# Seven half-block products over 12 instead of 8 of the 22 inner chunks of a down projection, and two weight parts queued behind the last sum of squares

## The chip, the cores and the metric

The kernel runs on one core of a Trainium2 chip. The metric is device time in microseconds (us); three runs of the kernel before gave a median of 2041.5 us (2040.48 to 2044.54). Engines are named as the profile names them: PE is TensorE (matmuls), PEld its loading of stationary operands, DVE is VectorE, ACT ScalarE, POOL GpSimd, SP SyncE, which here only issues transfers. Each engine works through its own queue in order, and so does each queue of transfers.

## The reference

An encoder trunk of two layers on 512 positions with 1024 features, in float32:

```python
for i in range(DEPTH):
    h = h + 0.5 * swiglu(rmsnorm(h, norm_ffn1[i]), ffn1_w_gate[i], ffn1_w_up[i], ffn1_w_down[i])
    hn = rmsnorm(h, norm_mix[i])
    if i % 2 == 0:
        h = h + ab_mixer(hn, ...)     # windowed and dilated attention
    else:
        h = h + c_mixer(hn, ...)      # 2-D neighbourhood attention
    h = h + 0.5 * swiglu(rmsnorm(h, norm_ffn2[i]), ffn2_w_gate[i], ffn2_w_up[i], ffn2_w_down[i])
    gate = jax.nn.sigmoid(rmsnorm(h, norm_ple[i]) @ w_ple_gate[i])
    h = h + gate * (p[i] @ w_ple_proj[i])
return rmsnorm(h, norm_final)

def swiglu(x, w_gate, w_up, w_down):          # inner width 2816 = 22 x 128
    return (silu(x @ w_gate) * (x @ w_up)) @ w_down
```

The last line of `swiglu` holds the down projection, which there are four of: 22 inner chunks of 128 rows go into 8 output chunks of 128 features, over 512 positions.

## The kernel before

Activations lie with features on the partitions, in chunks of 128 x 512. A float32 matmul is made of three in the format fp32r: each operand is split into a high part (a copy by ACT, L149) and a low part (the difference, by DVE, L150), and high x high, high x low and low x high are added up in PSUM. Weights come in units of 128 x 1024 (8 chunks) and pass through three rings of buffers: five raw ones (`wr`), four for high parts (`wh`), four for low parts (`wl`). A unit's parts can be written when TensorE is done with the unit four places before; a raw unit can be fetched when the parts of the one five places before are made. There are 8 buffers `tmp` of 128 x 512, 62 (`ACTS`) activation tiles `act`, and PSUM banks in pools: three `mm`, two `sc`, two `tr`, one `ob`. A planner lays each engine's queue out ahead of the run, by program order among what it takes to be ready, and sets all waits.

The trunk is TensorE's work from end to end: gate and up projections (`pair_front` for the first four pairs, `pair`, then `pair_fast`, in half-block products of its own), `down`, a mixer, and so on.

**Load phase.** `setup` starts the first norm. `pair_front` for m = 0 of the first feed-forward multiplies chunk by chunk as the input arrives, makes the weight parts of the second pair ahead, and then takes the squares and their sum (`norm_square`: a square on ACT, L207; a sum into `ssq`, on DVE in this first norm, L214). From the sum `stat` makes the column of factors (L221 on PE, L223 on DVE, L224 on POOL), and `spread` and ACT (L240, L248) make R of it, which every eviction (L281, L283) and `halves` (L314 and on) multiply by. The parts of the third pair (m = 2) are made by `unit` like all others.

**Feed-forward.** For each of 22 pairs the product r = silu(gate) * up is split into parts `a[m]`; for m < 8 r itself is also written to DRAM (`raw`, a POOL transfer, L408).

**Down.** Output chunks go in pairs (m, m+1). The first pair is `plain`: units of 8, 8 and 6 inner chunks, each chunk three matmuls of 512 columns (L438 to L440). While it runs, `inner_sums` makes, for k = 0 to 3, four differences (L515) of halves of chunk k and chunk k+4 fetched back from DRAM, and splits them; one result takes the place of the right half of `a[k]`. The three pairs that follow take inner chunks 0 to 7 by a two-by-two block scheme (inner chunks k and k+4, output chunks m and m+1, left and right 256 columns) that needs seven products instead of eight, each of 4 chunks x 3 matmuls of 256 columns (L476 to L478), and chunks 8 to 21 by `plain` units of 8 and 6. `inner_weights` makes the sums of weights for the seven products (L529 to L533) and four units of parts. The seven products come first in each pair; L482 to L494 join their results, then come the plain units, which add to the two banks of the outputs, and `evict` (L443) adds a bank into h, stores h to DRAM (`kept`, L444) and calls `norm_chunk`: the split of h for the next phase (L199, L200), and square and sum (L207, and L214 on POOL). For output chunks 3, 4, 5 (`LATER`) that norm is put off: in the last pair, between the seven products and the plain units, h is fetched again from `kept` (L430) and normed then.

Of the kernel before, what the change touches and what calls it, by code (L numbers as in the profile page):

```python
# [9 lines left out]
F32 = mybir.dt.float32  # L10
# [26 lines left out]
SEVEN = 4  # L37
LATER = 3, 4, 5
UP_AT = 3
LEAD = 6  # L40
ACTS = 62
# [6 lines left out]
class Trunk:  # L48
# [113 lines left out]
    def unit(self, src, cols=UNIT, lo_eng=None):  # L162

        nc = self.nc
        raw, hi, lo = self.unit_tiles()
        nc.sync.dma_start(raw[:, :cols], src)
        self.split(raw[:, :cols], hi[:, :cols], lo[:, :cols], lo_eng)
        return hi, lo
# [35 lines left out]
    def norm_square(self, c):  # L204
# [7 lines left out]
        else:  # L212
            eng = nc.vector if c == KC - 1 or self.k == 0 else nc.gpsimd
            eng.tensor_tensor(self.acc, self.acc, sq, op=ALU.add)  # L214
# [37 lines left out]
    def pair_front(self, w, m, first, ahead):  # L252
# [3 lines left out]
        for j in range(2):  # L256
            u = self.ahead.pop(0) if self.ahead else self.unit(w[:, (1 - j) * UNIT:(2 - j) * UNIT])
# [132 lines left out]
    def ffn(self, i, which, k_next):  # L390
# [8 lines left out]
        raw = self.dp.tile([2 * SEVEN, P, T], F32, name=self.nm("inner"))  # L399
        for m in range(NF):  # L400
# [6 lines left out]
            if m < 2 * SEVEN:  # L407
                nc.gpsimd.dma_start(raw[m], r)  # L408
# [9 lines left out]
    def down(self, w, a, raw, kept):  # L418

# [6 lines left out]
        later = []  # L426
# [6 lines left out]
        def plain(p, m, s, e, start):  # L433
            u = self.unit(w[m, :, s * P:e * P], (e - s) * P)
            for j, (xh, xl) in enumerate(a[s:e]):
# [4 lines left out]
                mm(p, u[1][:, c], xh, start=False, stop=s + j == NF - 1, skip_group_check=True)  # L440
# [20 lines left out]
        for m in range(2, KC, 2):  # L461
            hs = [fetched(m + j, kept) for j in range(2)]
            wa, wb, ws, wr = self.inner_weights(w[m, :, :UNIT], w[m + 1, :, :UNIT])
            M = UNIT // 2
            p1, p2, y, z = self.bank(), self.bank(), self.sbank(), self.obank()
            x11 = [(h[:, l], lo[:, l]) for h, lo in a[:SEVEN]]
            x21, x22 = [[(h[:, c], lo[:, c]) for h, lo in a[SEVEN:2 * SEVEN]] for c in (l, r)]
            t4 = [(h[:, r], lo[:, r]) for h, lo in a[:SEVEN]]
            t1, t2 = [[(h[:, c], lo[:, c]) for h, lo, _ in sums] for c in (l, r)]
            t3 = [(t[:, l], t[:, r]) for _, _, t in sums]  # L470

            def product(out, u, off, xs, start=False, stop=False):
                mm = nc.tensor.matmul
                for k, (xh, xl) in enumerate(xs):
# [950 lines left out]
```

## Time and profile before

| What | Value |
|---|---|
| median of three runs | 2041.5 us |
| time of the profiled execution | 2042.86 us |
| its span in the trace | 2041.1 us |
| mean granted TensorE clock | 0.997 |

The profile is of one execution. Its page gives the busy time of each engine, the chain of work that ended last, and groups of instructions as "line, engine, operation, output<-input, shapes xcount | busy us, mean ns | idle before, and what ended it". A timeline lists one engine's instructions with start, busy time, and in brackets the idle time before and its releaser; "x6" stands for six merged in one row. Matmuls overlap in the pipeline, so their pitch is read from starts. A table of windows gives per stretch: its length, then for PE, PEld, DVE, ACT and POOL the busy us with the count, then granted clock, share of the DMA engines, GB/s.

### The profile page before, as it was taken

What the parts mean: (1) busy time and instruction counts of PE and PEld (TensorE: products, weight loads), DVE (VectorE), ACT (ScalarE), POOL (GpSimd) and SP (SyncE); (2) the same over time, 40 slices, a digit from 0 to 9 for tenths busy, and PEclk for the clock granted to TensorE, in tenths of its full rate; (3) what the DMA queues carried; (4) which work ended last, traced back from release to release, by engine and by line L of the source; (5) the groups of instructions that cost most, each with busy time, mean ns of one, the idle gap of its engine ahead of it and who ended that gap; (6) DMA issues with size and microseconds to landing.
All of it is one profiled execution on the core that took longest, in us unless ns stands there. A gap on an engine that the chain in (4) does not pass through costs nothing.

```text
span 2041.1 us, 33721 instructions
## 1 busy us (share of the span) xinstructions
PE 2019.5 (99%) x12862; PEld 1820.6 (89%) x12862; DVE 1520.3 (74%) x2575; ACT 1056.9 (52%) x1798; POOL 260.2 (13%) x294
## 2 busy tenths in 40 slices
PE   9999999999999999999999999999999999999997
PEld 6999988878888899988888999888888889998886
DVE  7888865598766988875668888756788688888554
ACT  6555533377644555552445555434666545555242
POOL 0100011342212110000211100002000111000021
PEclk9999999999999999999999999999999999999999
DMA  7777644553425576653545775645343447665451
GB/s 212 193 188 188 181 139 157 150 104 73 100 73 165 137 195 182 170 191 124 185 150 159 192 183 158 201 125 161 109 112 102 155 134 192 184 179 165 132 193 42
DMA packets 123123, 312.94 MB, mean 153 GB/s; under 512 B 23504, under 2 KB 31184, under 8 KB 122960
## 3 DMA queue, kind: packets, MB, share of 16 engines
q1 hardware_dynamic: 104064, 253.06, 38.3%
q0 software_dynamic: 18752, 57.69, 15.0%
q8 instruction: 101, 1.65, 0.3%
q14 instruction: 62, 0.51, 0.1%
q10 hardware_dynamic: 144, 0.04, 0.0%
HBM read 274.02 MB, written 25.66 MB: 147 GB/s over the span
## 4 chain that ended last, share of the span: by engine, by line
PE 90%; DVE 3%; DMA 2%; ACT 2%; issue 1%; POOL 1%; SPq 0%; DVEq 0%; POOLq 0%; ACTq 0%
PE mm L362 6%; PE mm L361 6%; PE mm L360 6%; PE mm L174 6%; PE mm L438 6%; PE mm L439 6%; PE mm L173 6%; PE mm L440 6%; PE mm L175 6%; PE sc L362 3%; PE sc L361 3%; PE sc L360 3%; PE sc L175 3%; PE sc L173 3%; PE sc L174 3%; PE ob L360 2%
## 5 line engine op out<-in xcount | busy, mean ns | idle before, releaser
L149 ACT ACTIVATE wh<-wr 128x1024 fp32r<-128x1024 f32 (+2 forms) x455 | 466.2, 1026 | 541.5 <-PE mm L439 170.7
L150 DVE TENSOR_TENSOR wl<-wr,wh 128x1024 fp32r<-128x1024 f32 (+2 forms) x455 | 542.8, 1196 | 203.6 <-ACT wh L149 198.1
L362 PE MATMUL mm<-act,wl 128*128 128x256 f32 x1088 | 307.9, 283 | 0.0
L361 PE MATMUL mm<-act,wh 128*128 128x256 f32 x1088 | 307.9, 283 | 0.0
L360 PE MATMUL mm<-act,wh 128*128 128x256 f32 x1088 | 307.9, 283 | 0.0
L173 PE MATMUL mm<-act,wh 128*128 128x512 f32 (+1 forms) x648 | 254.4, 393 | 0.9 <-ACT act L149 0.4
L174 PE MATMUL mm<-act,wh 128*128 128x512 f32 (+1 forms) x648 | 254.2, 392 | 0.7 <-DVE act L200 0.6
L175 PE MATMUL mm<-act,wl 128*128 128x512 f32 (+1 forms) x648 | 253.3, 391 | 0.0
L361 PEld LDWEIGHTS mm<-act,wh 128*128 128x128 f32 x1088 | 208.9, 192 | 0.4
L362 PEld LDWEIGHTS mm<-act,wl 128*128 128x128 f32 x1088 | 208.9, 192 | 0.2
L360 PEld LDWEIGHTS mm<-act,wh 128*128 128x128 f32 x1088 | 208.9, 192 | 0.2
L438 PE MATMUL mm<-act,wh 128*128 128x512 f32 x512 | 199.4, 389 | 0.0
L439 PE MATMUL mm<-act,wh 128*128 128x512 f32 x512 | 199.4, 389 | 0.0
L440 PE MATMUL mm<-act,wl 128*128 128x512 f32 x512 | 199.2, 389 | 0.0
L149 ACT ACTIVATE act<-tmp 128x512 fp32r<-128x512 f32 (+1 forms) x204 | 113.7, 590 | 83.0 <-DVE tmp L515 33.1
L360 PE MATMUL sc<-act,wh 128*128 128x256 f32 x544 | 154.0, 283 | 0.0
L361 PE MATMUL sc<-act,wh 128*128 128x256 f32 x544 | 154.0, 283 | 0.0
L362 PE MATMUL sc<-act,wl 128*128 128x256 f32 x544 | 154.0, 283 | 0.0
L174 PEld LDWEIGHTS mm<-act,wh 128*128 128x128 f32 x648 | 122.2, 189 | 24.5 <-DVE act L200 2.2
L173 PEld LDWEIGHTS mm<-act,wh 128*128 128x128 f32 x648 | 121.9, 188 | 23.9 <-ACT act L199 0.8
L175 PEld LDWEIGHTS mm<-act,wl 128*128 128x128 f32 x648 | 122.1, 188 | 22.1 <-DVE wl L150 0.2
L150 DVE TENSOR_TENSOR act<-tmp,act 128x512 fp32r<-128x512 f32 (+1 forms) x200 | 125.7, 643 | 9.7 <-ACT act L149 7.7
(224 smaller groups left out, 4430.0 us busy)
## 6 DMA issues: line engine op xcount, KB each, us to landing
wr<-in_gu_dram SPq DMA_DIRECT2D x176, 512.0 KB, 4.7
wr<-in_gu_dram POOLq DMA_DIRECT2D x68, 512.0 KB, 5.5
wr<-in_dn_dram SPq DMA_DIRECT2D x64, 512.0 KB, 3.9
rb<-in_gu_dram SPq DMA_DIRECT2D x68, 256.0 KB, 3.0
wr<-in_dn_dram SPq DMA_DIRECT2D x32, 384.0 KB, 3.2
wr<-in_qk_ab_dram SPq DMA_DIRECT2D x20, 512.0 KB, 3.3
tmp<-kept SPq DMA_DIRECT2D x36, 256.0 KB, 4.1
inner<-tmp POOLq DMA_DIRECT2D x32, 256.0 KB, 3.6
```

Source lines behind the costliest of these rows:

```text
L149: self.put(self.nc.scalar.activation(hi, src, AF.Copy))
L150: self.put((lo_eng or self.nc.vector).tensor_tensor(lo, src, hi.bitcast(F32), op=ALU.subtract))
L173: mm(out, stat[0], mov[0], start=start, stop=False)
L174: mm(out, stat[0], mov[1], start=False, stop=False)
L175: return mm(out, stat[1], mov[0], start=False, stop=stop)
L360: mm(out, w[0][:, c], xs[k][0][:, x], start=start and k == 0, stop=False, skip_group_check=True)
L361: mm(out, w[0][:, c], xs[k][1][:, x], start=False, stop=False, skip_group_check=True)
L362: mm(out, w[1][:, c], xs[k][0][:, x], start=False, stop=stop and k == half - 1, skip_group_check=True)
L438: mm(p, u[0][:, c], xh, start=start and j == 0, stop=False, skip_group_check=True)
L439: mm(p, u[0][:, c], xl, start=False, stop=False, skip_group_check=True)
L440: mm(p, u[1][:, c], xh, start=False, stop=s + j == NF - 1, skip_group_check=True)
```

## The change

- `TWO` names six pairs of inner chunks: (0, 4), (1, 5), (2, 6), (3, 7), (8, 10), (9, 11). The seven products now cover inner chunks 0 to 11, with 6 chunks each. `raw` holds 12 chunks. `inner_sums` runs six times per down, for a pair once the first output pair's unit with its chunks has been issued.
- `plain` covers chunks 12 to 21, in two units of 5 (`others`).
- `inner_weights` fetches 1024 + 512 columns of both outputs (the 512 into the two buffers `rb` of `pair_fast`) and fills six units of parts instead of four.
- In the second output pair (m = 2) the plain units come first and the seven products after them; in the third and fourth pair the seven products come first, as before.
- The norm of output chunks 1 to 5 instead of 3 to 5 is put off to the last pair. `ACTS` goes from 62 to 64.
- In the load phase the parts of the third pair's two units are queued behind the last sum of squares (DVE's instructions among them; `issue_after` orders instructions on one engine).

```diff
-SEVEN = 4
-LATER = 3, 4, 5
+TWO = (0, 4), (1, 5), (2, 6), (3, 7), (8, 10), (9, 11)
+SEVEN = 12
+LATER = 1, 2, 3, 4, 5
-ACTS = 62
+ACTS = 64
...
-    def unit(self, src, cols=UNIT, lo_eng=None):
+    def unit(self, src, cols=UNIT, lo_eng=None, behind=None):
...
-        self.split(raw[:, :cols], hi[:, :cols], lo[:, :cols], lo_eng)
+        with self.tc.issue_after(behind.ins) if behind else ExitStack():
+            self.split(raw[:, :cols], hi[:, :cols], lo[:, :cols], lo_eng)
...
-            eng.tensor_tensor(self.acc, self.acc, sq, op=ALU.add)
+            self.last_sum = eng.tensor_tensor(self.acc, self.acc, sq, op=ALU.add)
...
-            u = self.ahead.pop(0) if self.ahead else self.unit(w[:, (1 - j) * UNIT:(2 - j) * UNIT])
+            u = self.ahead.pop(0) if self.ahead else self.unit(
+                w[:, (1 - j) * UNIT:(2 - j) * UNIT], behind=self.last_sum if first and m == 2 else None)
...
-            if m < 2 * SEVEN:
+            if m < SEVEN:
                 nc.gpsimd.dma_start(raw[m], r)
...
+        def others(p, m, start, stop):
+            mid = (SEVEN + NF) // 2
+            plain(p, m, SEVEN, mid, start, False)
+            plain(p, m, mid, NF, False, stop)
...
         for s in range(0, NF, 8):
+            e = min(NF, s + 8)
             for m in range(2):
-                plain(ps[m], m, s, min(NF, s + 8), s == 0)
-            if s == 0:
-                sums = [self.inner_sums(k, a, raw) for k in range(SEVEN)]
+                plain(ps[m], m, s, e, s == 0, e == NF)
+            sums += [self.inner_sums(k, k2, a, raw) for k, k2 in TWO if s <= max(k, k2) < e]
...
+        def seven(m, p1, p2, first, hs):
+
+            a11, a12, a22, s1, s2, s3, s4 = self.inner_weights(w[m], w[m + 1])
+            y, z = self.sbank(), self.obank()
             e, f, u2 = self.tmp(), self.tmp(), self.tmp()
+            product(y[:, l], a11, x11, True)
             act(e[:, l], y[:, l], AF.Copy)
+            product(p1[:, l], a12, x21, first)
+            product(p2[:, l], a22, t4, first, not first)
+            product(z[:, l], s1, t1, True, True)
+            product(y[:, r], s3, t3)
+            product(p1[:, r], s4, x22, False, not first)
+            product(y[:, l], s2, t2, False, True)
             act(u2[:, l], y[:, l], AF.Copy)
...
+        for m in range(2, KC, 2):
+            hs = [fetched(m + j, kept) for j in range(2)]
+            ps = self.bank(), self.bank()
+
+            first = m > 2
+            if first:
+                seven(m, *ps, True, hs)
             if m == KC - 2:
                 for c in later:
                     self.h[c] = fetched(c, self.kept)
                     self.norm_chunk(c)
+            for j, p in enumerate(ps):
+                others(p, m + j, not first, first)
+                if first:
+                    evict(m + j, p, hs[j])
+            if not first:
+                seven(m, *ps, False, hs)
+                for j, p in enumerate(ps):
+                    evict(m + j, p, hs[j])
...
     def inner_weights(self, w1, w2):
+        nc, dma, tt = self.nc, self.nc.sync.dma_start, self.nc.vector.tensor_tensor
+        M, G = UNIT // 2, UNIT // 4
...
+        for n, s in ((UNIT, 0), (M, UNIT)):
+            for x in (w1, w2):
+                raws.append(tile(self.wr, "wr", F32) if n == UNIT else
+                            self.tp.tile([P, T], F32, tag="rb", name=self.nm("rb"), bufs=2))
+                dma(raws[-1], x[:, s:s + n])
+        ra, rs, ra2, rs2 = raws
...
+        (ga,), (gb, b22) = parts(ra), parts(ra2, rs[:, M:])
         tt(rs[:, M:], rs[:, :M], rs[:, M:], op=ALU.add)
         tt(rs[:, :M], ra[:, :M], rs[:, :M], op=ALU.subtract)
+        (gs,) = parts(rs)
+        hi, lo = tile(self.wh, "wh", F32R), tile(self.wl, "wl", F32R)
+        self.split(rs2[:, G:], hi[:, :G], lo[:, :G])
+        tt(rs2[:, G:], rs2[:, :G], rs2[:, G:], op=ALU.add)
+        tt(rs2[:, :G], ra2[:, :G], rs2[:, :G], op=ALU.subtract)
+        self.split(rs2, hi[:, G:G + M], lo[:, G:G + M])
...
         tt(ra[:, :M], rs[:, M:], ra[:, :M], op=ALU.subtract)
         tt(ra[:, M:], ra[:, M:], ra[:, :M], op=ALU.subtract)
+        (gr,) = parts(ra)
+        tt(ra2[:, :G], rs2[:, G:], ra2[:, :G], op=ALU.subtract)
+        tt(ra2[:, G:], ra2[:, G:], ra2[:, :G], op=ALU.subtract)
+        (gr2,) = parts(ra2)
+        return (ga[:4] + gb[:2], ga[4:] + gb[2:], b22 + d22, gs[4:] + d1, gr[:4] + gr2[:2], gs[:4] + d3,
+                gr[4:] + gr2[2:])
```

More of the change, by code (lines that the diff above doesn't have):

```diff
@@ new lines, in inner_weights, with parts @@
+        raws = []
+        for n, s in ((UNIT, 0), (M, UNIT)):
[4 more added lines that the diff above has]
+        ra, rs, ra2, rs2 = raws
+        def parts(*srcs):
+            hi, lo, out, n = tile(self.wh, "wh", F32R), tile(self.wl, "wl", F32R), [], 0
+            for x in srcs:
+                c = slice(n, n + x.shape[-1])
+                self.split(x, hi[:, c], lo[:, c])
+                out.append([(hi[:, i:i + P], lo[:, i:i + P]) for i in range(c.start, c.stop, P)])
+                n = c.stop
+            return out
```

67 lines of the change are left out of this document (19 added, 48 removed).

## The prediction

> **What bounds the kernel now.** I read the page first: busy times, then the chain that ended last.
>
> ```profile
> span 2041.1 us, 33721 instructions
> PE 2019.5 (99%) x12862; PEld 1820.6 (89%) x12862; DVE 1520.3 (74%) x2575; ACT 1056.9 (52%) x1798; POOL 260.2 (13%) x294
> ...
> PE 90%; DVE 3%; DMA 2%; ACT 2%; issue 1%; POOL 1%; SPq 0%; DVEq 0%; POOLq 0%; ACTq 0%
> ...
> tmp<-kept SPq DMA_DIRECT2D x36, 256.0 KB, 4.1
> ```
>
> TensorE is busy for all but 2041.1 - 2019.5 = 21.6 us. So a matmul taken away shortens the kernel, and a wait put in front of TensorE lengthens it; work on VectorE, ScalarE or a queue counts only where TensorE comes to wait for it. Next, the first down projection by its four pairs of output chunks (window; then busy us and count of PE, PEld, DVE, ACT, POOL):
>
> ```profile
> 239.66:269.60 29.94, 29.94 (x134) 24.79 (x133) 24.39 (x45) 12.97 (x23) 0.58 (x1) 1.00 0.54 180
> 269.60:298.75 29.15, 29.15 (x169) 25.84 (x168) 17.54 (x21) 10.55 (x14) 4.68 (x4) 1.00 0.49 155
> 298.75:327.80 29.05, 29.05 (x169) 25.79 (x168) 15.09 (x19) 8.29 (x10) 1.10 (x2) 1.00 0.43 137
> 327.80:356.90 29.10, 29.10 (x170) 25.80 (x169) 18.61 (x19) 13.48 (x18) 7.43 (x6) 1.00 0.56 182
> ```
>
> TensorE never pauses here and its granted clock is 1.00. VectorE is filled to 24.39 of 29.94 us while the inner sums are made, to 15 to 19 of 29 afterwards. That is the room in which the change must put its new work. The pitch of matmuls stands in TensorE's timeline (start, busy; the starts are what counts, since busy times overlap):
>
> ```profile
> 271.04 0.28 PE L476 MATMUL mm<-act,wh 128*128 128x256 f32 x1
> ...
> 279.68 0.40 PE L438 MATMUL mm<-act,wh 128*128 128x512 f32 x1
> ...
> 298.75 0.28 PE L476 MATMUL sc<-act,wh 128*128 128x256 f32 x1
> ```
>
> From 271.04 to 279.68 lie six products of 12 half-width matmuls: 8.64/72 = 0.120 us each. From 279.68 to 298.75 lie 84 full-width ones: 19.07/84 = 0.227 us each.
>
> **Part 1, the seven products over 12 chunks.** Four more chunks for two outputs were 4 x 2 x 3 = 24 full matmuls, 24 x 0.227 = 5.45 us. They become 7 x 2 x 3 = 42 half ones, 42 x 0.120 = 5.04 us. That is 0.41 us saved per pair, and with three pairs in each of four downs 12 x 0.41 = **4.9 us off TensorE**, all of it on the path. [...]
>
> The price on the other engines, from the groups of instructions by shape:
>
> ```profile
> L150 DVE TENSOR_TENSOR wl<-wr,wh 128x1024 fp32r<-128x1024 f32 x406 | 501.4, 1237 | 184.5 <-ACT wh L149 179.0 <-PE mm L477 2.0 <-PE sc L175 1.7
> L150 DVE TENSOR_TENSOR act<-tmp,act 128x512 fp32r<-128x512 f32 x168 | 113.9, 685 | 8.5 <-ACT act L149 7.5
> L150 DVE TENSOR_TENSOR act<-tmp,act 128x256 fp32r<-128x256 f32 x32 | 13.4, 420 | 1.2 <-ACT act L149 0.2
> L515 DVE TENSOR_TENSOR tmp<-tmp,tmp 128x256 f32<-128x256 f32 x48 | 18.2, 421 | 1.6 <-DMA tmp<-inner 1.4
> ```
>
> An inner sum costs VectorE 4 x 0.42 (L515) + 2 x 0.42 + 0.69 = 3.2 us; two more per down are 6.4 us. Weights of a pair: four more sums of 256 columns (1.7 us), parts of 512, 256, 512 and 512 (0.69 + 0.42 + 0.69 + 0.69 = 2.5 us); the plain units hold 4 x 640 columns instead of 2 x 1024 and 2 x 768, at the first row's rate -1.2 us. So some +3 us in 29. In the first stretch the load would be 24.4 + 6.4 = 31 us, over 29.94; but the first pair now runs its plain part first (60 x 0.227 = 13.6 us), so there are 43.5 us for the 31, the plain units' 4 x 0.78 = 3.1 and the 3 of the weights, 37 in all. Cost taken: nothing, under the cover of VectorE's free quarter; if the sums ran late, the fourth product would wait for them (bound 6.4 us a down). ScalarE, at 13 of 30, takes its halves of the same parts. Four more stores of r per feed-forward on POOL's queue (POOL is at 13%) and four more fetches per down on SP, each ahead of weight loads that TensorE needs 20 us later: nothing. Nor do two more activation tiles cost time.
>
> **Part 2, the new join.** After the plain-first pair the next pair starts with seven products again, directly behind seven products. Its third product writes a PSUM bank that the pair before still holds until its first eviction. With three such banks, that eviction must land within two products, 36 x 0.120 = 4.3 us. The queue in front of it, from VectorE's timeline at the same place of the kernel before:
>
> ```profile
> 281.52 0.42 DVE L490 TENSOR_TENSOR tmp<-ob,tmp 128x256 f32<-128x256 f32 x1
> ...
> 283.24 0.69 DVE L494 SCALAR_TENSOR_TENSOR tmp<-tmp,tmp 128x512 f32<-128x512 f32 x1
> ...
> 289.43 0.69 DVE L443 SCALAR_TENSOR_TENSOR tmp<-mm,tmp 128x512 f32<-128x512 f32 x1 [1.99 <-PE mm L440]
> 290.76 0.69 DVE L529 TENSOR_TENSOR wr<-wr 128x512 f32<-128x512 f32 x1
> ...
> 292.03 1.79 DVE L530 TENSOR_TENSOR wr<-wr,wr 128x512 f32<-128x512 f32 x1
> ```
>
> And from ScalarE's, the copy that L490 waits for, and the first half of a norm:
>
> ```profile
> 266.52 0.71 ACT L199 ACTIVATE act<-tmp,gain 128x512 fp32r<-128x512 f32 x1
> ...
> 280.51 0.37 ACT L489 ACTIVATE tmp<-sc 128x256 f32<-128x256 f32 x1
> ```
>
> L490 to L494 take 283.93 - 281.52 = 2.4 us, the eviction 0.69, the copy with what it waits 0.5: 3.6 us, which fits by 0.7 us. If one weight part of 1.24 us gets between, it is late by 0.5 us; with the two of 512 columns as well, by 1.3. Nothing to 1.3 us per down; I take 0.2, since each queue is laid out by program order among what is ready, and evictions stand ahead of the later weights: **+0.8 us** in all.
>
> **Part 3, the end of a down.** Output chunks 1 to 5 instead of 3 to 5 have their norm put off to the last pair: a fetch from DRAM on SP, two ScalarE and one VectorE instruction, one sum on POOL each. The stretch after the last seven products shrinks from 19.07 to 13.6 us. SP's timeline in the kernel before:
>
> ```profile
> 340.33 1.30 SPq L430 DMA_DIRECT2D tmp<-kept  x2
> 345.75 0.33 SPq L166 DMA_DIRECT2D wr<-in_qk_ab_dram  x1
> 346.13 0.43 SPq L430 DMA_DIRECT2D tmp<-kept  x1
> ```
>
> The third fetch stands behind a weight load (L166) that waits for its buffer. Five fetches can stand behind three such loads. The fetch takes 4.1 us (first fence); the next phase needs chunk k only k x 24/8 x 0.227 = 0.68k us after its start, 3.4 us for chunk 5. If the fifth is issued 13 us into the 13.6, it lands at 17.1 and its parts (0.71 on ScalarE, 0.75 on VectorE) are ready at 18.6, against 13.6 + 3.4 = 17.0: 1.6 us late. If it is issued with the fourth, at 10, it is in time. TensorE can meanwhile take the first chunks of the next weight units. Nothing to 1.6 us; I take 0.2 per down, **+0.8 us**.
>
> **Part 4, the load phase.** VectorE's and TensorE's timelines:
>
> ```profile
> 17.82 4.67 DVE L214 TENSOR_TENSOR ssq<-ssq,tmp 128x512 f32<-128x512 f32 x6
> 22.41 1.22 DVE L150 TENSOR_TENSOR wl<-wr,wh 128x1024 fp32r<-128x1024 f32 x1
> 23.54 0.68 DVE L214 TENSOR_TENSOR ssq<-ssq,tmp 128x512 f32<-128x512 f32 x1
> 24.15 1.22 DVE L150 TENSOR_TENSOR wl<-wr,wh 128x1024 fp32r<-128x1024 f32 x1
> 25.37 0.16 DVE L223 TENSOR_SCALAR ms<-tr 128x4 f32<-128x4 f32 x1
> ```
>
> ```profile
> 24.28 1.05 PE L221 MATMUL tr<-ones,ssq 128*128 128x1 f32 x8 [1.00 <-DVE ssq L214]
> ...
> 26.41 0.63 PE L174 MATMUL mm<-act,wh 128*128 128x512 f32 x1
> 26.84 0.63 PE L175 MATMUL mm<-act,wl 128*128 128x512 f32 x1
> ...
> 53.39 0.50 PE L175 MATMUL sc<-act,wl 128*128 128x512 f32 x1 [0.43 <-DVE wl L150]
> ```
>
> ```profile
> 20.00:40.00 20.00, 19.00 (x83) 15.45 (x82) 15.75 (x28) 9.83 (x15) 3.22 (x4) 0.91 0.66 151
> 40.00:60.00 20.00, 19.57 (x88) 16.07 (x87) 19.82 (x33) 10.43 (x15) 1.44 (x2) 1.00 0.47 120
> ```
>
> The third pair's part at 22.41 delays the last sum by 23.54 - 22.41 = 1.1 us. TensorE idles 1.00 us for it and then runs at a pitch of 0.43 instead of 0.227 us; the clock of the slice is 0.91, so 20 x 0.09 = 1.8 us are lost. On TensorE alone up to 1.0 + 1.8 = 2.8 us could come back. But from 40 to 60 VectorE is busy 19.82 of 20, and TensorE at 53.39 waits for it; so what counts is how much earlier VectorE's own row of work starts, after L223. The matmuls between L221 and the transposes that spread R then run at 0.227, which I count as 0.6 us; L223 itself comes 1.1 us earlier if it runs ahead of the second part, and not at all if both parts, which now queue behind the last sum, come first. So VectorE gains 0.6 to 1.7 us. What TensorE gains beyond that turns into a longer wait at 53.39. Bounds: 2.8 us gained; 0.6 lost, if the longer wait brings the slow pitch again (1.8) and VectorE gains 1.2. I take the middle of 0.6 and 1.7, **-1.2 us**.
>
> **Sum.** -4.9 + 0.8 + 0.8 - 1.2 = -4.5 us. The profiled execution ran 2042.86 us, 1.8 over its span of 2041.1; by it the change gives 2038.4. The median of the runs is 2041.5, 1.4 below it, so the forecast against the median is **2037.0 us**. A measurement of this kernel can tell about 0.2%, 4.1 us, from no change; the forecast lies 0.4 us beyond that bound.
>
> **The rivals.**
> *The joins eat it (same).* Each new join is late by the 1.3 us of part 2: 4 x 1.3 = 5.2 instead of 0.8, 2041.4 us. For it: weights precede in time while the eviction is not ready; against: no wait of TensorE stands anywhere in the downs before.
> *The late norms (slower).* One mechanism: the fetches of chunks 1 to 5 go out one by one behind weight loads. If the fourth and the fifth each stand behind another load, the loads being freed every 15 x 0.227 = 3.4 us, the fifth goes out at 16.4, is ready at 22.0 and TensorE waits 5 us per down: 2037.0 - 0.8 + 20 = 2056 us. It turns the verdict once a down loses (4.5 + 0.8 + 4.1)/4 = 2.4 us. For it: the 4.5 us from the end of the second fetch's issue to the third. Against: other units' first chunks can fill in.
> *POOL slows VectorE (same or a little slower).* L530 took 1.79 us where L529 just before took 0.69; POOL began a sum at 291.56:
>
> ```profile
> 291.56 1.71 POOL L214 TENSOR_TENSOR ssq<-ssq,tmp 128x512 f32<-128x512 f32 x1 [0.58 <-ACT tmp L207]
> ```
>
> That is 1.1 more. Two more sums in the shorter last stretch are 2.2 us of VectorE per down; if all reaches TensorE, 8.8 us, 2045.8 us; VectorE's 18.61 of 29.10 speaks against. [...]
> *The load phase gives nothing (same).* The longer wait at 53.39 brings the slow pitch again: 2037.0 + 1.2 + 0.6 = 2038.8 us.
>
> **How the numbers follow.** Forecast 0.50 (its own range 2034.0 to 2038.5, of which 0.42 lies below 2037.4, the bound of faster); joins 0.20; late norms 0.12; POOL 0.08; load 0.10. Of joins and load 0.05 is faster, where the other part goes better than taken, and 0.25 the same; POOL splits into 0.05 the same and 0.03 slower. Faster 0.47, same 0.08 + 0.25 + 0.05 = 0.38, slower 0.15. The range, 2033.8 to 2043.5, goes from all of part 4 (2.8) with no join loss, 2041.5 - 4.9 - 2.8, past the joins case, and leaves out the late norms and most of the POOL case.
>
> **What would show it.** Right: half-width matmuls in the downs at 0.120, each pair 28.7 us; the first L221 near 23.2 with no wait; few waits of TensorE at the third product of the second pair. Wrong: TensorE waiting for L443's successor or for a put-off norm at the end of each down, a clock below 1.00 in slices there, or a wait at 53 us that has grown beyond 1.5 us.

## The result and the profile after

The changed kernel took 2052.2 us in the median of 6 runs (2050.7 to 2058.8), the kernel before 2042.0 beside it: ratio 1.0054, interval 1.0043 to 1.0065. It is slower by 10 us, where 4.5 us faster was forecast. First the page of the changed kernel:

```profile
span 2051.2 us, 34574 instructions
PE 2022.2 (99%) x13078; PEld 1831.3 (89%) x13078; DVE 1566.1 (76%) x2727; ACT 1079.4 (53%) x1870; POOL 266.8 (13%) x310
```

TensorE is still the path, yet it is busy for 2.7 us more with less to do, and idle for 29.0 us instead of 21.6. Its mean granted clock is 0.994 instead of 0.997, which fits busy time that grows while there is less to multiply. To find the place, cut both spans where a down begins and ends (first and last `plain` matmul) and take a table of windows over the pieces (first the stretch, then its length and TensorE's busy time). Kernel before:

```profile
0.00:239.66 239.66, 235.56 (x1692) 220.25 (x1693) 199.60 (x294) 137.12 (x211) 20.64 (x30) 0.99 0.69 188
239.66:357.03 117.37, 117.37 (x638) 102.33 (x637) 75.62 (x104) 45.32 (x66) 13.78 (x13) 1.00 0.50 163
357.03:877.55 520.52, 516.19 (x3358) 460.68 (x3356) 405.00 (x783) 298.19 (x580) 99.82 (x122) 1.00 0.52 135
...
994.92:1279.20 284.28, 283.96 (x1933) 263.74 (x1932) 222.90 (x332) 153.26 (x228) 33.19 (x36) 1.00 0.61 170
...
1396.57:1852.39 455.82, 454.12 (x3037) 416.74 (x3036) 356.09 (x698) 265.78 (x488) 37.67 (x42) 1.00 0.52 145
...
1969.76:2041.10 71.34, 60.15 (x303) 49.92 (x301) 34.58 (x56) 21.43 (x31) 13.26 (x12) 0.94 0.27 93
```

And the changed kernel:

```profile
0.00:238.18 238.18, 234.54 (x1693) 218.98 (x1693) 199.66 (x295) 137.11 (x211) 23.92 (x34) 1.00 0.70 193
238.18:354.47 116.29, 116.29 (x693) 103.97 (x691) 82.25 (x137) 47.00 (x78) 7.39 (x10) 1.00 0.53 173
354.47:878.63 524.16, 517.17 (x3357) 461.39 (x3356) 411.67 (x789) 301.67 (x586) 108.40 (x130) 1.00 0.52 138
...
994.93:1284.13 289.20, 287.21 (x1933) 265.69 (x1932) 226.61 (x336) 156.73 (x234) 41.51 (x44) 0.99 0.60 172
...
1400.42:1860.81 460.39, 455.80 (x3037) 417.73 (x3036) 361.27 (x703) 269.26 (x494) 44.16 (x50) 1.00 0.52 147
...
1977.10:2051.20 74.10, 62.35 (x303) 51.58 (x301) 37.27 (x59) 25.05 (x37) 19.68 (x16) 0.91 0.27 93
```

The four downs alike went from 117.37 to 116.29 us, busy throughout: 4 x 1.08 = 4.3 us won. The stretch ahead of the first down became 1.5 us shorter. All that turned the result lies in the four stretches behind a down, which hold the same matmuls as before: 3.64 + 4.92 + 4.57 + 2.76 = 15.9 us. The sum, -4.3 - 1.5 + 15.9 = +10.1, is the difference of the spans.

What waits there stands in the changed kernel's list of TensorE's waits (total us, times, longest):

```profile
PE tr L242 <- POOL rcol L226: 5.9, 4, 1.7
...
PE mm L176 <- DVE act L202: 2.0, 4, 1.2
PE sc L175 <- ACT act L201: 1.8, 1, 1.8
```

L201 and L202 are the split of a norm, L226 and L242 the column of factors that comes of the finished sum of squares and its spreading into R. The row of 1.8 us is behind the first down, at 359.12: there it is the split of the fourth put-off chunk itself that comes late. Behind the four downs TensorE's waits make 2.1, 2.0, 2.9 and 1.7 us, 8.7 in all (two of the rows hold waits of the load phase too); in the kernel before they make 0, 0.2, 0 and 0.8. The rest of the 15.9 shows behind the second down, in TensorE's timeline:

```profile
1003.54 0.50 PE L176 MATMUL mm<-act,wh 128*128 128x512 f32 x1 [0.27 <-DVE act L202]
...
1007.49 1.11 PE L242 MATMUL tr<-ident,rcol 128*128 128x128 f32 x4 [1.72 <-POOL rcol L226]
1008.26 0.78 PE L175 MATMUL mm<-act,wh 128*128 128x512 f32 x1
...
1009.26 0.63 PE L177 MATMUL mm<-act,wl 128*128 128x512 f32 x1
...
1013.10 0.62 PE L177 MATMUL sc<-act,wl 128*128 128x512 f32 x1
```

In the kernel before, the same matmuls of L242 (there L240) came without a wait:

```profile
1004.55 0.65 PE L240 MATMUL tr<-ident,rcol 128*128 128x128 f32 x4
```

Here there is a pause of 1.72 us, and then the next ten matmuls start every 0.43 us (1009.26 to 1013.10 are nine pitches) instead of 0.227, at half the clock (granted 0.50 from 1006.76 to 1013.59). The twelve matmuls from 1008.26 to 1013.52 take 5.26 us instead of 12 x 0.227 = 2.7, which is 2.5 us, so the pauses (2.0) and the slow piece together are most of the 4.92. Why the norms are late is seen in SP's queue at the same place:

```profile
983.65 0.39 SPq L432 DMA_DIRECT2D tmp<-kept  x1
987.05 0.33 SPq L167 DMA_DIRECT2D wr<-in_plg_dram  x1
987.47 0.38 SPq L432 DMA_DIRECT2D tmp<-kept  x1
990.45 0.33 SPq L167 DMA_DIRECT2D wr<-in_plp_dram  x1
990.88 0.40 SPq L432 DMA_DIRECT2D tmp<-kept  x1
993.85 0.33 SPq L167 DMA_DIRECT2D wr<-in_plg_dram  x1
994.22 0.42 SPq L432 DMA_DIRECT2D tmp<-kept  x1
```

The last four of the five fetches (L432) go out one by one, each behind a weight load (L167), 3.3 to 3.8 us apart; the fifth leaves 0.7 us before the down ends. Its norm and those of the last chunks then crowd VectorE and POOL (both engines' timelines):

```profile
1000.45 3.04 DVE L202 SCALAR_TENSOR_TENSOR act<-tmp,gain,act 128x512 fp32r<-128x512 f32 x2 [0.38 <-ACT act L201]
1003.41 0.68 DVE L216 TENSOR_TENSOR ssq<-ssq,tmp 128x512 f32<-128x512 f32 x1
...
999.94 2.99 POOL L216 TENSOR_TENSOR ssq<-ssq,tmp 128x512 f32<-128x512 f32 x2 [0.92 <-ACT tmp L209]
```

The last sum is done at 1004.09, 9.2 us behind the down; in the kernel before it was done at 998.48, 3.6 us behind:

```profile
997.79 0.69 DVE L214 TENSOR_TENSOR ssq<-ssq,tmp 128x512 f32<-128x512 f32 x1
```

### The profile page after: what moved, and what is told of

It is laid out like the page before. It is cut to its first block, busy times and chain, and to the rows that moved or that the text cites. A ratio compares the mean times of both kernels' runs of the same rounds, so it can differ in the third digit from the quotient of the medians.

```text
span 2051.2 us, 34574 instructions
## 1 busy us (share of the span) xinstructions
PE 2022.2 (99%) x13078; PEld 1831.3 (89%) x13078; DVE 1566.1 (76%) x2727; ACT 1079.4 (53%) x1870; POOL 266.8 (13%) x310
## 4 chain that ended last, share of the span: by engine, by line
PE 91%; DVE 3%; ACT 2%; DMA 2%; issue 1%; POOL 1%; SPq 0%; DVEq 0%; POOLq 0%; ACTq 0%
PE mm L365 6%; PE mm L364 6%; PE mm L363 6%; PE mm L175 6%; PE mm L176 6%; PE mm L177 6%; PE mm L440 4%; PE mm L441 4%; PE mm L442 4%; PE sc L365 3%; PE sc L364 3%; PE sc L363 3%; PE sc L177 3%; PE sc L176 3%; PE sc L175 3%; PE ob L365 2%
## 5 line engine op out<-in xcount | busy, mean ns | idle before, releaser
L150 ACT ACTIVATE wh<-wr 128x1024 fp32r<-128x1024 f32 (+3 forms) x455 | 454.8, 1003 | 438.5 <-DVE wr L353 81.9
L151 DVE TENSOR_TENSOR wl<-wr,wh 128x1024 fp32r<-128x1024 f32 (+3 forms) x455 | 526.6, 1162 | 160.8 <-ACT wh L150 136.5
L150 ACT ACTIVATE act<-tmp 128x512 fp32r<-128x512 f32 (+1 forms) x228 | 123.7, 578 | 110.7 <-DVE tmp L532 55.5
L440 PE MATMUL mm<-act,wh 128*128 128x512 f32 x416 | 162.0, 389 | 0.0
L441 PE MATMUL mm<-act,wh 128*128 128x512 f32 x416 | 162.0, 389 | 0.0
L442 PE MATMUL mm<-act,wl 128*128 128x512 f32 x416 | 161.8, 389 | 0.0
L151 DVE TENSOR_TENSOR act<-tmp,act 128x512 fp32r<-128x512 f32 (+1 forms) x224 | 137.6, 631 | 12.4 <-ACT act L150 8.8
```

The costliest lines, as they stand in the source:

```text
L150: self.put(self.nc.scalar.activation(hi, src, AF.Copy))
L151: self.put((lo_eng or self.nc.vector).tensor_tensor(lo, src, hi.bitcast(F32), op=ALU.subtract))
L440: mm(p, u[0][:, c], xh, start=start and j == 0, stop=False, skip_group_check=True)
L441: mm(p, u[0][:, c], xl, start=False, stop=False, skip_group_check=True)
L442: mm(p, u[1][:, c], xh, start=False, stop=stop and j == e - s - 1, skip_group_check=True)
```

## The experiments

Three theories: **A**, the number of norms put off against the length of the last products (19.1 us before, 13.6 after) sets the end, through the chain of fetches; **B**, POOL's sums of squares beside VectorE lengthen it; **C**, something else behind the down ends last, and the norms only look like it. All ratios below are to the kernel before on the same chip, with their interval. "Gaps" are the four stretches behind the downs, less those of the profiled kernel before; each is of one execution, and in other versions of the kernel before, with three chunks put off, they lie between -1.4 and +0.5, so that much is scatter.

**The load phase alone**, in the kernel before (`behind` and its use, nothing else).

> The kernel before with the load-phase edit alone. In the changed kernel the first down starts 1.48 us earlier than before (238.18 against 239.66) and nothing else changed ahead of it. Both theories: the span is 1.5 us shorter, ratio 0.9993, the first L223 (the sum over partitions) near 23.2 us, the granted clock of 20 to 40 us back at 1.00. If the gain is lost later, the time is unchanged.

2043.0 us, 1.0006 (0.9997 to 1.0015): nothing that can be told. The first stretch was 238.98 us here. But it was 238.04 in the next kernel, which lacks this edit, and 239.76 in a later one, which has it: what decides about it is told below, with part 4.

**Five chunks put off, alone**, in the kernel before:

```diff
-LATER = 3, 4, 5
+LATER = 1, 2, 3, 4, 5
```

> The kernel before with the norms of output chunks 1 to 5 instead of 3 to 5 put off; 8 chunks in the seven products, so the stretch behind the last seven products keeps its 19.07 us. Theory A (the five fetches go out one at a time, each behind the square of the chunk before in the order of the tmp buffers and so behind a weight load that waits 3.4 to 5.4 us): the fifth fetch goes out some 19 us into the stretch, TensorE loses 2 to 4 us after each down, 2042 + 8 to 16 = 2050 to 2058 us. Theory B (six sums on POOL, and VectorE beside them, do not fit into the 13.6 us of the changed kernel): with 19 us and POOL busy 7.4 of 29 us they fit, at most 1 us per down, 2042 to 2046 us.

2054.5 us, 1.0062 (1.0049 to 1.0076); gaps +1.4, +3.8, +5.1, +4.2, together 14.5 of the 15.9 us. One constant, without the new products and with the old 19.1 us, reproduces the loss. VectorE's last sum behind the second down:

```profile
998.84 3.04 DVE L200 SCALAR_TENSOR_TENSOR act<-tmp,gain,act 128x512 fp32r<-128x512 f32 x2 [0.38 <-ACT act L199]
1001.80 0.68 DVE L214 TENSOR_TENSOR ssq<-ssq,tmp 128x512 f32<-128x512 f32 x1
```

**All fetches first**, in the changed kernel, to break the chain:

```diff
 for c in later:
     self.h[c] = fetched(c, self.kept)
+for c in later:
     self.norm_chunk(c)
```

> The changed kernel with all five fetches issued ahead of the five norms instead of one fetch and one norm in turn; the work of every engine is the same. Theory A: the five fetches stand together in SP's queue, the fifth chunk lands some 10 us earlier, the 15.9 us lost after the four downs (3.6, 4.9, 4.6, 2.8) shrink to 0 to 4, so 2052 - 12 to 16 = 2036 to 2040 us. Theory B: POOL and VectorE have the same work in the same stretch, 2048 us or more.

2066.0 us, 1.0119 (1.0105 to 1.0132): worse. The fetches did leave together, but the norms then stand in a block, ahead of the weight parts:

```profile
992.22 6.43 POOL L216 TENSOR_TENSOR ssq<-ssq,tmp 128x512 f32<-128x512 f32 x4
...
991.07 6.43 DVE L202 SCALAR_TENSOR_TENSOR act<-tmp,gain,act 128x512 fp32r<-128x512 f32 x4
```

Four splits take VectorE 6.43 us instead of 4 x 0.75 = 3.0 beside POOL, and the next weight part comes only behind them. Breaking the chain of fetches alone does not help.

**The five sums on VectorE** instead of POOL, in the changed kernel:

```diff
-eng = nc.vector if c == KC - 1 or self.k == 0 else nc.gpsimd
+eng = nc.vector if c == KC - 1 or self.k == 0 or (self.k % 2 and 0 < c < 6) else nc.gpsimd
```

> The changed kernel with the sums of squares of chunks 1 to 5 after each down on VectorE (0.69 us each) instead of POOL (1.3 to 2.2 us each). Theory A: the fifth chunk still lands late; only the last sums get shorter, by some 1.5 us per down, 2046 to 2052 us. Theory B: POOL is out of the way, 10 us or more come back, 2042 us or less.

2048.4 us, 1.0035 (1.0023 to 1.0048): 3.8 us back. That lies in the range expected under A (2046 to 2052) and far from B's (2042 or less): POOL's sums are a part of the loss and not the whole.

**Squares early**, in the changed kernel: squares and sums at the eviction, only fetch and split late:

```diff
 if m in LATER:
     later.append(m)
+    self.norm_square(m)
...
-    self.norm_chunk(c)
+    self.norm_split(c)
```

> The changed kernel with square and sum of the put-off chunks made at their eviction, as for the others; put off to the last pair are only the fetch and the split of h, since only the split needs activation tiles. Theory A' (the put-off norms reach the path by two ways: the fetches go out one at a time because a square's buffer lies between them, and, once they do not, five sums on POOL and VectorE's splits beside them queue up in front of the last chunk): both are gone, the 15.9 us behind the downs shrink to 0 to 4, the down projections keep their 4.3 us: 2041.4 - 4.3 + 0 to 4 = 2036 to 2041 us. Theory C (the shorter stretch of 13.6 us itself is the cause, for whatever work lies there): 2047 us or more.

2053.8 us, 1.0057 (1.0043 to 1.007): nothing back, where 2036 to 2041 was expected if squares and chain were all. No trace shows an execution of this length; what the nothing is made of can be read from two later kernels with the same edit (Seven products first; Squares early and p early).

**Fetches first and sums on VectorE**, both edits:

> Fetches issued together as in e3, and the sums of chunks 1 to 5 on VectorE as in e4. Theory A': e3 lost by POOL's and VectorE's instructions lengthening each other (four splits took 6.43 us); without POOL they take 3 us, the last chunk's eviction comes 4 us earlier, 2040 to 2048 us. If e3's loss came from the order of the queues (the weights' parts behind all the norms), it stays above 2055 us.

2048.2 us, 1.0030 (1.0018 to 1.0041): no more than the sums alone. But the block of norms no longer costs: without POOL beside them the splits take 0.74 us each. So the four that took 6.43 were lengthened by POOL's sums.

**Squares early in the kernel before**, where three chunks are put off:

> The kernel before with square and sum of its put-off chunks 3 to 5 made at their eviction. If the put-off sums cost it nothing (no wait of TensorE behind its downs except about 1 us at the two embeddings), 2040.5 to 2042 us; it shows whether a gain of e5 is the change's or the earlier sums'.

2040.7 us, 0.9997 (0.9988 to 1.0005): free there.

**Seven products first** in the second pair too, with squares early (`first = True`):

> e5 with the second output pair in the order of the others: seven products first. The prediction holds that the plain-first order is needed because the inner sums fill VectorE (31 us of work for 29.94 us). If so TensorE waits at the first seven products by 1 to 6 us per down, 4 to 24 us over e5; if the sums fit anyway, the same as e5 within 1 us, or up to 0.8 us less, since the join of seven behind seven goes from the first of three pairs.

2054.0 us, 1.0055 (1.004 to 1.0071). The downs are together 7.1 us longer than in the changed kernel: TensorE waits 0.9 to 2.0 us in each for VectorE's weight parts (L151), so the plain-first order had its reason. The gaps are +0.7, +4.6, +0.9 and +3.6: squares early cured them behind the first and the third down. Behind the second and the fourth the trace showed the place of theory C. SP's queue and TensorE behind the second down (which ends at 996.7 here):

```profile
996.42 0.33 SPq L167 DMA_DIRECT2D wr<-in_plg_dram  x1
996.80 0.90 SPq L1248 DMA_DIRECT2D tmp<-in_pT_dram  x2
...
1003.11 0.50 PE L175 MATMUL sc<-act,wh 128*128 128x512 f32 x1 [0.81 <-ACT act L150]
1004.46 0.66 PE L176 MATMUL sc<-act,wh 128*128 128x512 f32 x1 [0.85 <-POOL act L151]
```

All norms are done by 1000.3, but TensorE now waits for the split of p, the per-layer input that the next phase multiplies. Its fetch (L1248) stands in SP's queue behind a weight load. In the changed kernel (first row; there L1247) it goes out 4.1 us behind the down, in the kernel before (second row; L1209) half a us ahead of the down's end:

```profile
999.05 0.80 SPq L1247 DMA_DIRECT2D tmp<-in_pT_dram  x2
...
994.44 0.86 SPq L1209 DMA_DIRECT2D tmp<-in_pT_dram  x2
```

So two things end these two stretches, one behind the other; behind the first and the third down no p is fetched. The next kernels separate them. The early fetch of p is this edit:

```diff
 # last pair of the down, ahead of the late fetches
+self.p_raw = [self.tp.tile([P, T], F32, tag="rb", name=self.nm("rb"), bufs=2) for _ in self.next_p]
+for x, src in zip(self.p_raw, self.next_p):
+    nc.sync.dma_start(x, src)
...
-raw = self.tmp()
-nc.sync.dma_start(raw, io["pT"][i, :, c, :])
-p.append(self.split_chunk(raw))
+p.append(self.split_chunk(self.p_raw[c]))
```

**Squares early and p early**, in the changed kernel:

> The changed kernel with the squares of the put-off chunks taken at their evictions (so that only the fetch and the two splits of a chunk are late) and with the two halves of the next part's per-layer input fetched ahead of the five late fetches, into two tiles of their own tag. In the kernel with seven products first, the stretches behind the second and the fourth down projection stood on the split of this input (fetched at 996.80 behind a weight load, landed at 1002.4, against 994.44 and 998.4 in the kernel before) and then ran at half the granted clock. If two things end these stretches one after the other (first the chain of late norms, then the late input), both are now taken away, the gaps behind the second and the fourth down come back to within 1.5 us of before, and the time is about 2042 us (downs -4.3, the two other stretches up to +4). If neither matters beside the plain amount of late work, it stays at 2052 to 2054 us. If even the stretches behind the first and third down recover, it is about 2038 us.

2045.1 us, 1.0013 (1.0005 to 1.0022). The gaps are back: +0.7, +0.1, +0.8, -1.5. Five chunks are fetched late here too, but without the squares between them the fetches leave together:

```profile
984.10 2.29 SPq L433 DMA_DIRECT2D tmp<-kept  x5
```

What remains is new and lies inside the downs, which take 117.98 us instead of 116.29, at one wait in each. TensorE, VectorE and POOL there:

```profile
947.60 0.39 PE L479 MATMUL ob<-act,wh 128*128 128x256 f32 x1 [1.42 <-ACT wh L150]
...
943.31 1.02 DVE L573 TENSOR_TENSOR rb<-rb 128x256 f32<-128x256 f32 x1
...
945.38 1.50 DVE L574 TENSOR_TENSOR rb<-rb,rb 128x256 f32<-128x256 f32 x1
...
942.73 1.30 POOL L216 TENSOR_TENSOR ssq<-ssq,tmp 128x512 f32<-128x512 f32 x1
...
944.55 2.05 POOL L216 TENSOR_TENSOR ssq<-ssq,tmp 128x512 f32<-128x512 f32 x1
```

Two sums of weights, 0.42 us each alone, take 1.02 and 1.50 beside POOL's sums of chunks 2 and 3: 1.7 us, and the down is 1.7 us longer. That also explains why squares early alone gave nothing, as far as it can be read from this trace and that of seven products first: what it wins behind the first and the third down (+3.6 and +4.6 become +0.7 and +0.8), these 4 x 1.7 = 6.8 us take away again.

**p early alone**, in the changed kernel:

> The changed kernel with only the early fetch of the two halves of the per-layer input, the late norms left as they are. If the chain of late norms ends the stretches by itself (the sum of squares is complete only at about 1001 us behind the second down), nothing comes back: 2051 to 2053 us. If the input's fetch was the real end and the norms only look like it, 5 to 7 us come back: 2045 to 2047 us.

2048.1 us, 1.0031 (1.002 to 1.0043): 4 us back, between the two expectations. Its fastest execution, the one in the trace, has gaps of +2.3, +1.2, +3.3 and 0.0: there p early helps most behind the second and the fourth down, where p is fetched.

**p early in the kernel before:**

> Control: the kernel before with the early fetch of the per-layer input alone. There the pauses behind the second and the fourth down are 0.22 and 0.83 us, on the split of this input, so at most 1 us can come back: 2040 to 2042 us. Above 2043 us would say that the early fetch itself harms, and the two runs beside it have to be read against that.

2040.0 us, 0.999 (0.9981 to 0.9999): a small gain by itself.

**Four chunks put off**, in the kernel before (`LATER = 2, 3, 4, 5`):

> The kernel before with four chunks put off (2 to 5) instead of three; five cost 13 us. If each chunk beyond three costs the same, this takes half: about 2047 to 2048 us. If there is a cover that three and four still fit and five exceed, it takes less than 2 us: at most 2043.5 us. If the first extra chunk already breaks the cover, it takes 10 us or more.

2042.4 us, 1.0002 (0.9993 to 1.0011): nothing. So the loss is a step between four and five at 19.1 us, as a cover that runs out. The last sum behind the second down, to be held against that of five above:

```profile
997.76 0.68 DVE L214 TENSOR_TENSOR ssq<-ssq,tmp 128x512 f32<-128x512 f32 x1
```

Done at 998.4 (down's end 994.4, 4.1 us behind) against 1002.5 (994.7, 7.7 behind).

The kernels that follow are the changed kernel with p early and one thing more.

**Four put off in the changed kernel**, with `ACTS = 66`, `WR = 4`:

> The changed kernel with the early fetch of the per-layer input, four put-off chunks instead of five (chunk 1 is normed at its eviction again), its two further activation tiles paid for by four raw weight tiles instead of five. Four put-off chunks cost nothing in the kernel before; here they have 13.6 us of other products instead of 19.1. If the fifth chunk alone broke the cover, the downs' 4.3 us are kept and the time is 2040.0 - 4.3 = 2035.7 us (2034 to 2038). If the shorter stretch breaks it with four as well, it is 2041 to 2048 us. Losing a raw weight tile costs an unknown amount everywhere; above 2050 us says that it does.

2051.0 us, 1.0047 (1.0034 to 1.0059); gaps +3.0, +3.7, +3.5, +2.3; the downs 116.28. Four fit 19.1 us and not the 13.6, as A has it, though this kernel also has four raw weight buffers instead of five, which was not tried by itself; with the same four, three put off leave no such gap (below).

**Ten chunks by products** (`TWO` without (9, 11), four put off):

> The changed kernel with ten inner chunks by products instead of twelve (five pairs; the second group has one pair), four put-off chunks, and the early fetch of the per-layer input, with five raw weight tiles as before. The weight sums of the sixth pair and the parts of one block are still computed, and not used. The downs should be about half way between 117.37 and 116.29 us, so -2.1 us in all. If four put-off chunks are covered: 2040.0 - 2.1 = 2038 us (2036.5 to 2039.5). If the shorter stretch (some 16 us here) breaks it: 2042 us or more.

2056.7 us, 1.0074 (1.006 to 1.0088): gaps of +4.0, +3.9, +4.8 and +0.5 with all five raw weight buffers, so four did not fit this stretch (some 16 us) either. The downs took 117.88 us, about 1 more than the counts of matmuls give; why stays open.

**Sums on VectorE:**

> The changed kernel with the early fetch of the per-layer input and the sums of squares of chunks 1 to 5 on VectorE instead of POOL, five chunks put off. The sums alone gave back 3.8 us and the early fetch alone 4. If they take away two different waits, both count: about 2044 us. If each only shortens the same stretch, it stays at 2047 to 2048 us.

2047.5 us, 1.0029 (1.0017 to 1.004): the two gains do not add.

**The square of chunk 1 alone early:**

> The changed kernel with the early fetch of the per-layer input and the square of chunk 1 alone taken at its eviction, at the start of the down where ScalarE has slack; chunk 1's fetch and splits stay late, chunks 2 to 5 are late whole. Taking all five squares early gave the stretches back whole but made each down 1.7 us longer. If the count of late squares and sums sets the end, one less of five gives back part: 2043 to 2046 us. If what costs is the fetch or the splits of the fifth chunk, nothing comes back beside the early fetch alone: 2047 to 2049 us.

2056.1 us, 1.0074 (1.0061 to 1.0086): worse than none early, outside all that was expected. TensorE waits four times for L201, 5.1 us in all; why this order is worse stays open.

**Squares of 2 and 3 behind the products**, squares early otherwise:

```diff
 if m in LATER:
     later.append(m)
-    self.norm_square(m)
+    if m not in (2, 3):
+        self.norm_square(m)
...
 seven(m, *ps, True, hs)
+if m == 4:
+    self.norm_square(2)
+    self.norm_square(3)
```

> The changed kernel with early squares and the early fetch of the per-layer input, as in the run that gave the four stretches back but lost 1.69 us in each down, at one place: a wait of 1.42 us for a weight split of the second set of seven products, behind VectorE operations of that set that took 1.02 and 1.50 us beside POOL's sums of chunks 2 and 3 (0.42 elsewhere). Here the squares and sums of chunks 2 and 3 come behind that set of seven products instead of ahead of it; nothing else is moved. If POOL's sums beside VectorE were the cause, the downs are 116.3 us again and the time is about 2045.0 - 6.8 = 2038 us (2036.5 to 2040.5), faster than both kernels. If the wait has another cause, or comes back at the next place, it stays at 2044 to 2046 us. If the two held chunks take the buffers that the products need, above 2047 us.

2038.1 us, 0.9983 (0.9974 to 0.9992): as expected, and faster than both kernels. Part of that is the early fetch of p, with which alone the kernel before took 2040.0 us; beside that kernel the gain is 1.4 us by the ratios, and the two intervals overlap. The same two operations on VectorE without POOL beside them:

```profile
941.22 0.41 DVE L577 TENSOR_TENSOR rb<-rb 128x256 f32<-128x256 f32 x1
...
942.69 0.42 DVE L578 TENSOR_TENSOR rb<-rb,rb 128x256 f32<-128x256 f32 x1
```

The downs take 116.29 us again, the gaps are +1.1, -0.5, +0.6, -1.7, and no granted clock behind a down is below 1.00 but in the tail.

**Three put off in the changed kernel**, with `ACTS = 68`, `WR = 4`, `TMPS = 6`:

> The changed kernel with the early fetch of the per-layer input and only three chunks put off (3 to 5), as in the kernel before; the four activation tiles more that this takes are paid for by four raw weight tiles instead of five and six temporary tiles instead of eight. If the number of chunks against the length of the last products is what counts (three at 19.1 us and four at 19.1 us fitted, five at 19.1 and four at 13.6 did not), three fit 13.6 us: no gap behind a down is more than 1 us over the kernel before for this reason, and with the smaller tile pools costing nothing the time is 2036 us. If the smaller pools cost, it is above that by waits on weight loads or temporaries that stand elsewhere too; at 2047 us or more with the waits on late splits still behind the downs, the count theory falls.

2043.7 us, 1.0009 (1.0 to 1.0018). The gaps are +1.2, +0.3, +1.1, -0.8, and behind no down does TensorE wait for a put-off split: three fit the 13.6 us. So theory A holds in this, that the number of norms put off against the stretch decides. That it does so through the chain of fetches is not shown: breaking the chain alone made things worse, and squares early, which cured the gaps, took the late squares and sums away together with the chain. The smaller pools cost elsewhere: 0.43 us in each down and 2.1 ahead of the first.

## Why the prediction was wrong

**Part 1 held.** -4.9 with +0.8 for Part 2 was -4.1; the downs gave -4.3, with no wait of TensorE inside them. VectorE carried 82.3 us per down instead of 75.6: the 6.6 more came out of its free quarter, as assumed, and are less than the 15 that the terms add up to (6.4 for the sums and 3 for each of three pairs). The rows' pitch was right: in the changed kernel's first down 126 half-width matmuls from 325.73 to 340.84 start every 0.120 us, and 60 full ones from 312.10 to 325.73 every 0.227.

**Part 2 held or was smaller:** nothing of the joins shows; taken was 0.2 per down.

**Part 3 is the step that failed.** It took 0.2 us per down with bounds of 0 and 1.6; measured 2.8 to 4.9. Its timing of the fifth fetch was not far off: that left 12.9 us after the stretch of 13.6 began (its bad end was 13), and the split was ready 5.1 us behind the down (it had 5.0). What it priced from there was wrong, three times. (Behind the first down the wait is of the kind it priced, 1.77 us for a put-off chunk's own split, that of the fourth.) It looked at what that chunk's products need, and not at what queues behind it: the splits of the last two chunks (the row of 3.04 us) and the last sum of squares, which needs all chunks, and with it R, which every eviction of the next phase waits for. Neither did it count POOL's sums against VectorE just there. And it priced a pause at its length, where here half clock came with a pause (granted 0.50 for 6.83 us): behind the second down 2.0 us of pauses cost 4.9. The rival "late norms" had the right place and size (2056, at 5 us per down; 2052.2 and 4.0 came) and too low a chance. It took the fetches for 3.4 us apart, as they were, but had the fifth out at 16.4 us, where it went at 12.9, and the 5 us came of what stood behind it; so its size is right by luck. That "other units' first chunks can fill in" was true and did not last: TensorE ran on for 8.3 us behind the second down before its first wait above 0.2 us, and behind the first for 2.9 us, and then the cover was gone.

The prediction also left out a transfer of the next phase behind the moved ones: p's fetch stands behind the weight loads that the moved norms delay. Removing that alone gave 4.0 us, removing squares alone nothing, both together 7.1 and the gaps whole. That is two things. Behind the second and the fourth down there are two waits, one hidden by the other: with squares early alone the gaps there stay at +4.6 and +3.6, with both they are +0.1 and -1.5. And squares early alone lost in the downs what it won behind the first and the third.

**Part 4 came out in number (-1.5 for -1.2), not in cause.** Two rows of the changed kernel show the beginning as forecast: the sums now run on without a weight part between (L216), and TensorE's wait is shorter (L223, 0.82 for 1.00):

```profile
17.70 5.46 DVE L216 TENSOR_TENSOR ssq<-ssq,tmp 128x512 f32<-128x512 f32 x7
...
23.22 1.05 PE L223 MATMUL tr<-ones,ssq 128*128 128x1 f32 x8 [0.82 <-DVE ssq L216]
```

No slow pitch follows, but that is not the edit's doing. The first stretch took 237.9 to 239.0 us in the nine traces whose granted clock stays at 1.00 there, and 239.1 to 239.8 in the nine in which half clock begins at about 25 us for 3.4 us (the kernel with smaller pools left out); the profiled kernel before, with 239.66, is one of these, at 0.50 from 25.96 to 29.37. Without the edit two of five are of the first kind, with it seven of thirteen, and the edit alone gained nothing. So the 1.5 us are a half-clock stretch that the profiled execution of the kernel before happened to have and this one not: luck.

**POOL beside VectorE**, the third rival, was real: it made the late splits twice as long (0.74 us each again where the sums ran on VectorE) and was 1.7 us per down in one run. In the rows both sides lengthen: a split from 0.74 to 1.5 us (the rows of 3.04 for two), POOL's sum from 1.30 to 2.05.

## What to carry to other kernels

Work moved to the end of a phase is measured against the cover there as a whole, and by the last thing that needs all of it (here the sum of squares), not by what each piece needs; count how many pieces go out at what interval (here five at 3.4 us against 13.6) and expect a step, not a slope (at 19.1 us four cost nothing, five 13 us). When taking one late thing away gives nothing, look at what the engine waits for then, there and in the stretches ahead, and take both away in one run. Price a pause of TensorE at one to two and a half times its length (behind the third down of the kernel with p early 3.0 us of pauses cost 3.3 and no half clock followed; behind the second of the changed kernel 2.0 us cost 4.9 with it).

## What was not expected of the hardware

The half clock after a pause does not follow from the pause alone. In the changed kernel a wait of 1.73 us for L226 (at 1413.55, behind the third down) was followed by pitches of 0.43 us until 1416.2. In the kernel with p early the same wait, 1.72 us, was not, and the granted clock stayed at 1.00 from 1405 to 1421; its TensorE rows:

```profile
1409.54 0.65 PE L242 MATMUL tr<-ident,rcol 128*128 128x128 f32 x4 [1.72 <-POOL rcol L226]
...
1410.50 0.39 PE L177 MATMUL mm<-act,wl 128*128 128x512 f32 x1
1410.73 0.39 PE L175 MATMUL mm<-act,wh 128*128 128x512 f32 x1
```

The stretch behind the third down was 459.1 us there, against 460.4, and that execution was the fastest of its kernel's six (2045.0 to 2051.4). The stretches of half clock have a step of their own, 3.41 us. In the changed kernel (window, its length, TensorE's busy us with the count, granted clock, share of the DMA engines, GB/s):

```profile
1006.76:1013.59 6.83, 6.10 (x17) 0.50 0.46 154
1412.95:1416.36 3.41, 2.81 (x9) 0.50 0.65 202
```

There, and in the traces of three kernels with p early (four put off in the changed kernel, sums on VectorE, the square of chunk 1 alone early), each stretch of half clock behind the second and the third down lasts 3.4 or 6.8 us, and the second of them begins a whole number of 3.413 us after the first: 406.19 us, 119 times, in the changed kernel, and 402.8, 402.8 and 406.2 us, 118, 118 and 119 times, in the three others. So these stretches begin at a step of their own, and where a pause falls on it would be chance. That would explain why the same pause came with half clock in one execution and not in another, and the wide scatter of kernels that pause, but it was not tested by itself. The pauses were short: no wait behind a down in the changed kernel was longer than 1.8 us, and in the 3.41 us ahead of these two stretches TensorE was busy for 2.23 and 2.29 us. Nor does that busy time alone decide: in the kernel with p early it was 1.7 us in the window from 1407.65 to 1411.06, and the clock stayed at 1.00. What brings the half clock stays open.
